# Seven-product feed-forward layers: two raw products ahead of the token sums, the sums made by halves, and the fourth layer by seven products too

## The chip, the cores and the metric

The kernel runs on one core of one Trainium2 chip. The metric is the device time of one execution in microseconds: the median of three runs of the unchanged kernel is compared with runs of the changed one. Everything is computed in fp32; a matrix product takes three matmuls, because both operands are split in a high and a low part (`hi = copy to fp32r`, `lo = x - hi`).

## The reference, cut to what matters

The network has two blocks. The change touches the second, which runs for `i = 0, 1`:

```python
def swiglu_ffn(x, w_in, w_out):
    h = x @ w_in
    g, u = jnp.split(h, 2, axis=-1)
    return (jax.nn.silu(g) * u) @ w_out

for i in range(2):
    x = layer_norm(a * x + 0.5 * swiglu_ffn(x, ffn_w_in[i, 0], ffn_w_out[i, 0]), ln_g[i, 0], ln_b[i, 0])
    h = diff_attention(x, ...) if i == 0 else pool_mixer(x, ...)
    x = layer_norm(a * x + h, ln_g[i, 1], ln_b[i, 1])
    x = layer_norm(a * x + memory_cross_attention(x, mem, ...), ln_g[i, 2], ln_b[i, 2])
    x = layer_norm(a * x + 0.5 * swiglu_ffn(x, ffn_w_in[i, 1], ffn_w_out[i, 1]), ln_g[i, 3], ln_b[i, 3])
```

There are 512 tokens, 1024 features, and 2816 hidden features, which makes 22 hidden units of 128. So there are four feed-forward layers; the text calls them F00, F01, F10 and F11, in the order in which they run. F10 stands between the two halves of the network: F01 ends just before it, and the pool mixer follows it.

## The kernel before

The engines of a core are TensorE (PE, with its weight loads PEld), VectorE (DVE), ScalarE (ACT), GpSimd (POOL) and SyncE (SP), whose queue issues nearly all loads. The kernel is written with tile pools; a planner orders each engine's instructions (by the order of the program, taking what it believes to be ready) and places the waits. Each engine then runs its list in order. Four token tiles of 128 tokens hold the activations `X`; `x_T` transposes one token tile on PE into PSUM, ACT copies the high half `xh` (L187) and DVE makes the low half `xl` (L188).

A layer is `ffn`. It works through the 22 units in chunks (6, 6, 6, 4 units, in F10 8, 7, 7). For each chunk it first makes the hidden units and then multiplies them by `w_out` into the residual, for two halves of the 1024 output columns; behind the second half of the last chunk comes the LayerNorm (`ln_tile`), one token tile after the other. Weights are made by a list of `steps`; `need(n, ahead=5)` makes all steps up to `n + ahead`: an SP load into one of three `wst` buffers (or one of four `sq`), a copy on ACT (`whi`, L168) and a subtraction on DVE (`wlo`, L169), each into one of six buffers.

Units 0 and 1 of a layer are plain: two products of 128 columns by 512 tokens each, taken in two halves of tokens, because the last token tile of `X` is still in its LayerNorm when the layer begins. `s.flush()` runs what is pending, the transpose of the last token tile, between the two halves; `finish` makes the hidden unit. In F00, F01 and F11 (`seven=True`) the other units go in pairs by a Strassen-Winograd scheme: seven products of 256 tokens with half the contraction length in place of eight. It needs sums of weights (`seven_units`: four DVE additions and seven splits a pair) and sums of tokens, made once a layer by `sums` after the flush: four additions `xh + xl` back to fp32 (L1112), four sums (L1120 to L1124), four splits (L1126, L1127). `products` issues the seven products and combines them on DVE and ACT. F10 has plain products for all units. PSUM has three banks `g`, two `a`, one `o` and two `t`.

`G` and `B`, the LayerNorm's rows, are loaded at the start of `ffn`; the constants of the pool mixer (`pool_open`: `band`, `bando`, `br`, `sr` and its own `G` and `B`) before F10 begins.

## Time and profile before

| what | us |
| --- | --- |
| median of 3 runs | 3044.82 (3042.84 to 3045.26) |
| the profiled execution, its own time | 3046.43 |
| its span, first to last instruction | 3044.6 |
| PE busy in it | 2931.4 (96%) |
| DVE busy in it | 2094.4 (69%) |
| ACT busy in it | 1262.4 (41%) |
| mean granted PE clock | 0.988 of full speed |

The span is what the trace shows; the execution's own time has a little more around it. Busy times are of instructions, and an engine that isn't on the path that sets the end may idle without cost. Matmul records overlap, since matmuls are pipelined: the distance from the start of one to the start of the next tells what one costs, not its own duration.

### The profile page before, as it was taken

What the parts mean: (1) busy time and instruction counts of PE and PEld (TensorE: products, weight loads), DVE (VectorE), ACT (ScalarE), POOL (GpSimd) and SP (SyncE); (2) the same over time, 40 slices, a digit from 0 to 9 for tenths busy, and PEclk for the clock granted to TensorE, in tenths of its full rate; (3) what the DMA queues carried; (4) which work ended last, traced back from release to release, by engine and by line L of the source; (5) the groups of instructions that cost most, each with busy time, mean ns of one, the idle gap of its engine ahead of it and who ended that gap; (6) DMA issues with size and microseconds to landing.
All of it is one profiled execution on the core that took longest, in us unless ns stands there. A gap on an engine that the chain in (4) does not pass through costs nothing.

```text
span 3044.6 us, 45001 instructions
## 1 busy us (share of the span) xinstructions
PE 2931.4 (96%) x17662; PEld 2566.0 (84%) x17662; DVE 2094.4 (69%) x3251; ACT 1262.4 (41%) x2159; POOL 434.4 (14%) x555
## 2 busy tenths in 40 slices
PE   8989999989998999999999989999999999999998
PEld 7778788878787999988888889998888888888997
DVE  6676755785766887688774687777333386687777
ACT  6435636545643344335544243333222224343332
POOL 1553510563510000011110000000000040000000
PEclk9999999999999999999999999999999999999999
DMA  5213134123132333321244233324323225223332
GB/s 187 69 57 103 39 131 164 56 61 103 46 118 82 112 117 106 96 97 57 63 147 130 79 109 91 97 91 146 103 93 95 91 77 153 70 95 100 104 97 70
DMA packets 93300, 296.99 MB, mean 98 GB/s; under 512 B 12320, under 2 KB 17952, under 8 KB 93088
## 3 DMA queue, kind: packets, MB, share of 16 engines
q1 hardware_dynamic: 92944, 293.85, 30.3%
q8 instruction: 140, 2.29, 0.3%
q14 instruction: 72, 0.59, 0.1%
q10 hardware_dynamic: 144, 0.26, 0.0%
HBM read 281.49 MB, written 12.58 MB: 97 GB/s over the span
## 4 chain that ended last, share of the span: by engine, by line
PE 74%; DVE 14%; DMA 4%; ACT 3%; issue 3%; POOL 1%; SPq 0%; DVEq 0%; ACTq 0%; POOLq 0%
PE g L176 52%; PE a L176 15%; PE o L176 5%; DVE wlo L169 3%; DVE X L283 1%; DMA wst<-in_ffn_w_in 1%; DMA wst<-in_w_in 1%; ACT whi L168 1%; PE t L246 1%; POOL rs_y L207 1%; PE t L1069 1%; DVE X L282 1%; DVE xl L188 1%; DMA sq<-in_ffn_w_in 1%; DVE nb L955 0%
## 5 line engine op out<-in xcount | busy, mean ns | idle before, releaser
L168 ACT ACTIVATE whi<-wst 128x1024 fp32r<-128x1024 f32 (+2 forms) x442 | 462.6, 1048 | 700.7 <-PE g L176 288.2
L169 DVE TENSOR_TENSOR wlo<-wst,whi 128x1024 fp32r<-128x1024 f32 (+2 forms) x435 | 535.1, 1234 | 316.2 <-ACT whi L168 301.7
L176 PE MATMUL g<-xh,whi 128*128 128x256 f32 (+1 forms) x1776 | 564.2, 318 | 2.1 <-ACT xh L187 1.5
L176 PE MATMUL g<-xl,whi 128*128 128x256 f32 (+1 forms) x1776 | 559.6, 315 | 1.3 <-DVE xl L188 1.1
L176 PE MATMUL g<-xh,wlo 128*128 128x256 f32 (+1 forms) x1776 | 559.7, 315 | 0.2 <-DVE wlo L169 0.2
L207 POOL TENSOR_TENSOR rs_y<-rs_a,mhalf 128x1 f32<-128x1 f32 (+4 forms) x90 | 99.1, 1101 | 2112.1 <-DVE rs_a L206 2110.6
L176 PE MATMUL g<-whi,xh 128*128 128x512 f32 (+2 forms) x960 | 365.5, 381 | 0.0
L176 PE MATMUL g<-wlo,xh 128*128 128x512 f32 (+2 forms) x960 | 358.7, 374 | 0.8 <-DVE wlo L169 0.8
L176 PEld LDWEIGHTS g<-xh,whi 128*128 128x128 f32 x1776 | 338.2, 190 | 23.6 <-ACT xh L187 2.9
L176 PE MATMUL g<-whi,xl 128*128 128x512 f32 (+2 forms) x960 | 358.0, 373 | 0.0
L176 PEld LDWEIGHTS g<-xh,wlo 128*128 128x128 f32 x1776 | 337.4, 190 | 21.3 <-DVE wlo L169 0.6
L176 PEld LDWEIGHTS g<-xl,whi 128*128 128x128 f32 x1776 | 337.0, 190 | 21.6 <-DVE xl L188 2.2
L176 PE MATMUL a<-xh,whi 128*128 128x256 f32 (+1 forms) x1008 | 305.1, 303 | 23.0 <-ACT xh L1126 22.6
L176 PE MATMUL a<-xl,whi 128*128 128x256 f32 (+1 forms) x1008 | 303.1, 301 | 0.0
L176 PE MATMUL a<-xh,wlo 128*128 128x256 f32 (+1 forms) x1008 | 303.0, 301 | 0.0
L168 ACT ACTIVATE whi<-sq 128x1024 fp32r<-128x1024 f32 x120 | 126.5, 1059 | 290.9 <-PE o L176 122.5
L176 PE MATMUL g<-whi,hh 128*128 128x512 f32 x547 | 217.2, 397 | 3.7 <-DVE h L1259 3.7
L176 PEld LDWEIGHTS a<-xh,whi 128*128 128x128 f32 x1008 | 194.1, 193 | 30.7 <-ACT xh L1126 23.2
L176 PE MATMUL g<-wlo,hh 128*128 128x512 f32 x547 | 216.3, 396 | 0.0
L176 PE MATMUL g<-whi,hl 128*128 128x512 f32 x547 | 216.3, 395 | 0.0
L176 PEld LDWEIGHTS g<-whi,xl 128*128 128x128 f32 x960 | 181.7, 189 | 30.4
L176 PEld LDWEIGHTS g<-wlo,xh 128*128 128x128 f32 x960 | 182.5, 190 | 29.4 <-DVE wlo L169 1.5
(389 smaller groups left out, 5602.1 us busy)
## 6 DMA issues: line engine op xcount, KB each, us to landing
wst<-in_ffn_w_in SPq DMA_DIRECT2D x146, 512.0 KB, 3.5
wst<-in_ffn_w_out SPq DMA_DIRECT2D x86, 512.0 KB, 3.6
wst<-in_w_in SPq DMA_DIRECT2D x64, 512.0 KB, 4.0
wst<-in_xa_wkv SPq DMA_DIRECT2D x32, 512.0 KB, 4.0
sq<-in_ffn_w_in SPq DMA_DIRECT2D x30, 512.0 KB, 3.5
wst<-in_da_w_qkv SPq DMA_DIRECT2D x24, 512.0 KB, 3.7
wst<-in_w_out SPq DMA_DIRECT2D x16, 512.0 KB, 3.5
wst<-in_w_pg SPq DMA_DIRECT2D x16, 512.0 KB, 4.4
```

Source lines behind the costliest of these rows:

```text
L168: s.nc.scalar.activation(hi[:, :n], st[:, :n], AF.Copy)
L169: (s.nc.gpsimd if s.lo_pool else s.nc.vector).tensor_sub(lw[:, :n], st[:, :n], hi[:, :n])
L176: s.nc.tensor.matmul(out, lhsT, rhs, start=start, stop=stop)
L188: nc.vector.tensor_sub(lo, ps, hi)
L207: nc.gpsimd.tensor_tensor(y, a, s.mhalf[:p].to_broadcast([p, n]), op=OP.pow)
L246: s.nc.tensor.transpose(ps[:, j], src[:, j * 128:(j + 1) * 128], s.ident)
L282: nc.vector.scalar_tensor_tensor(X[:, cs], X[:, cs], mv[:, 0:1], G[:, cs], op0=OP.subtract, op1=OP.mult)
L283: nc.vector.scalar_tensor_tensor(X[:, cs], X[:, cs], rs, B[:, cs], op0=OP.mult, op1=OP.add)
L1069: nc.tensor.transpose(pt[:, j], me["P"][:, j * 128:(j + 1) * 128], s.ident)
```

## The change

- `sums` gives back two functions, `fulls(z, n)` and `rest(z)`, for z = 0 and 1. Each works on half of each token half: z = 0 is token tiles 0 and 2, z = 1 is tiles 1 and 3. The intermediate sums lie in the buffers `h`, `U` and `sg` that `products` uses later, no longer in `wst` and `sq`.
- The order of the seven products becomes: both raw ones (of the two contraction halves of tokens 0 to 255) first, then four with token sums, with the raw one of tokens 256 to 511 between them. `seven_units` loads and splits the weights in that order.
- `begin` issues the two raw products of a pair. For the first pair of a layer it runs before the flush, with PSUM bank `o` for the second; after it come the sums of z = 0 and two additions of z = 1, then the flush, the rest of z = 1, the next weights, and `finish` of units 0 and 1.
- While the first units are made, weights are prepared 2 or 0 steps ahead in place of 5.
- `G`, `B` and `ST` are made at the last chunk. F10 has seven products and chunks of 6, 6, 6, 4; its work tiles lie in a pool `S` of their own on the right side of the memory, which is closed at the last chunk, and the pool mixer's constants are loaded then (`late`).

```diff
-        def full(*key):
-            f = s.stage().rearrange("p (k c) -> p k c", k=4)
-            nc.vector.tensor_add(f, *q[key])
-            return f
-
-        def summed():
-            return F.tile([128, UN], F32, name="sq", bufs=4).rearrange("p (k c) -> p k c", k=4)
-
-        st = [summed() for _ in range(4)]
-        a, b = full(0, 0), full(0, 1)
-        nc.vector.tensor_sub(st[0], a, b)
-        c = full(1, 1)
-        nc.vector.tensor_add(st[1], c, st[0])
-        nc.vector.tensor_sub(st[2], b, c)
-        nc.vector.tensor_sub(st[3], full(1, 0), st[1])
-        for n in (1, 2, 0, 3):
-            nc.scalar.activation(hi[:, n], st[n], AF.Copy)
-            nc.vector.tensor_sub(lo[:, n], st[n], hi[:, n])
+        full = [{}, {}]
+
+        def fulls(z, n):
+            zs = slice(128 * z, 128 * z + 128)
+            if n:
+                f = F.tile([128, 2, 512], F32, name="h", bufs=1).rearrange("p k (f c) -> p k f c", c=128)
+            elif z:
+                f = F.tile([128, 2, 512], F32, name="U", bufs=1).rearrange("p k (f c) -> p k f c", c=128)
+            else:
+                f = F.tile([128, 2, 2, 256], F32, name="sg", bufs=1).rearrange("p k a (b c) -> p k (a b) c", c=128)
+            for k in range(2):
+                full[z][k, n] = f[:, k]
+                nc.vector.tensor_add(f[:, k], *(y[:, :, zs] for y in q[k, n]))
+
+        def rest(z):
+            zs = slice(128 * z, 128 * z + 128)
+            f = full[z]
+            nc.vector.tensor_sub(f[0, 0], f[0, 0], f[0, 1])
+            nc.vector.tensor_sub(f[0, 1], f[0, 1], f[1, 1])
+            nc.vector.tensor_add(f[1, 1], f[1, 1], f[0, 0])
+            nc.vector.tensor_sub(f[1, 0], f[1, 0], f[1, 1])
+            for n, y in ((1, f[1, 1]), (2, f[0, 1]), (0, f[0, 0]), (3, f[1, 0])):
+                nc.scalar.activation(hi[:, n, :, zs], y, AF.Copy)
+                nc.vector.tensor_sub(lo[:, n, :, zs], y, hi[:, n, :, zs])
+
         t = [(hi[:, n], lo[:, n]) for n in range(4)]
-        return q[0, 0], t[1], t[2], t[0], q[1, 0], q[1, 1], t[3]
+        return fulls, rest, (q[0, 0], q[1, 0], t[1], t[2], t[0], q[1, 1], t[3])
...
         def u0():
             load(0, 0, s.stage())
+            return split(me[0, 0])
+
+        def u1():
+            load(0, 1, s.stage())
             load(1, 0, summed())
             load(1, 1, s.stage())
-            me["s3"] = summed()
+            return split(me[0, 1])
+
+        def u2():
+            me["s3"], me["s2"], me["s4"] = summed(), summed(), summed()
             nc.vector.tensor_add(me["s3"], me[0, 0], me[1, 0])
-            return split(me[0, 0])
-
-        def u1():
-            load(0, 1, s.stage())
-            me["s2"], me["s4"] = summed(), summed()
             nc.vector.tensor_add(me["s2"], me["s3"], me[1, 1])
             nc.vector.tensor_add(me["s4"], me["s2"], me[0, 1])
             return split(me["s2"])
 
-        def u3():
+        def u4():
             nc.vector.tensor_add(me[1, 0], me[1, 0], me[1, 1])
             return split(me[1, 0])
 
-        return [u0, u1, lambda: split(me["s3"]), u3, lambda: split(me[0, 1]), lambda: split(me["s4"]),
-                lambda: split(me[1, 1])]
-
-    def ffn(s, i, j, want_T, out=False, after=None, chunks=(6, 6, 6, 4), seven=False, room=None):
-        nc = s.nc
-        with s.scope(f"F{i}{j}") as P:
-            G, B = s.ln_rows(i, 3 * j, P)
-            ST = P.tile([128, 4, 2, 6], F32, name="ST")
+        return [u0, u1, u2, lambda: split(me["s3"]), u4, lambda: split(me["s4"]), lambda: split(me[1, 1])]
...
+    def ffn(s, i, j, want_T, out=False, late=None, chunks=(6, 6, 6, 4), room=None):
+        nc = s.nc
+        with s.scope(f"F{i}{j}") as P, ExitStack() as inside:
+            S = inside.enter_context(s.tc.tile_pool(name=f"S{i}{j}", bufs=1, side="right")) if late else P
+            hh, hl = (P.tile([128, max(chunks), 512], F32R, name=n) for n in ("hh", "hl"))
...
+            def mul(at, n, ps, ahead=5):
+
+                w = need(at + n, ahead)
+                b = ps().rearrange("p (j c) -> p j c", j=2)
+                for z in range(2):
+                    for k in range(4):
+                        s.mm3(b[:, z], tuple(x[:, k, z * 128:(z + 1) * 128] for x in w),
+                              (t7[n][0][:, k], t7[n][1][:, k]), k == 0, k == 3)
+                return b
+
+            def begin(at, ps=None, ahead=5):
+
+                p1 = S.tile([128, 2, 256], F32, name="p1", bufs=1)
+                nc.scalar.activation(p1, mul(at, 0, s.g, ahead), AF.Copy)
+                return p1, mul(at, 1, ps or s.a, ahead)
...
-                p1, U2, U3 = (P.tile([128, 2, 256], F32, name=n, bufs=1) for n in ("p1", "U2", "U3"))
-                nc.scalar.activation(p1, mul(0, s.g), AF.Copy)
-                nc.vector.tensor_sub(U2, mul(1, s.a), p1)
-                nc.vector.tensor_add(U3, mul(2, s.g), U2)
-                b = mul(3, s.a)
+                Us = S.tile([128, 2, 512], F32, name="U", bufs=1).rearrange("p n (j c) -> p n j c", j=2)
+                U2, U3 = Us[:, 0], Us[:, 1]
+                nc.vector.tensor_add(sg[:, 0], b, p1)
+                nc.scalar.activation(sg[:, 0], sg[:, 0], AF.Silu)
+                nc.vector.tensor_sub(U2, mul(at, 2, s.g), p1)
+                nc.vector.tensor_add(U3, mul(at, 3, s.a), U2)
+                b = mul(at, 4, s.g)
                 nc.vector.tensor_sub(h[:, 1], U3, b)
                 nc.vector.tensor_sub(U2, U2, b)
-                nc.vector.tensor_add(sg[:, 0], mul(4, s.g), p1)
-                nc.scalar.activation(sg[:, 0], sg[:, 0], AF.Silu)
-                nc.vector.tensor_sub(sg[:, 1], mul(5, s.a), U2)
+                nc.vector.tensor_sub(sg[:, 1], mul(at, 5, s.a), U2)
                 nc.scalar.activation(sg[:, 1], sg[:, 1], AF.Silu)
-                nc.vector.tensor_add(h[:, 0], mul(6, s.g), U3)
+                nc.vector.tensor_add(h[:, 0], mul(at, 6, s.g), U3)
...
+                if u0:
+                    hh, hl = (P.tile([128, max(chunks), 512], F32R, name=n) for n in ("hh", "hl"))
+                last = u0 + nu == FF // 128
+                begun = {}
                 if u0 == 0:
-                    for u, _, at in inner[:2]:
-                        first[u] = [part_of(at, s.g), part_of(at + 1, s.a)]
+                    first = []
+                    for u, at in inner[:2]:
+                        first.append([s.fm_part(need(at + z, 2), ps()) for z, ps in enumerate((s.g, s.a))])
                         for part in first[u]:
                             part(0, 256)
+                    fulls, rest, t7 = s.sums(room or S, S, xT)
+                    begun[2] = begin(inner[2][1], s.o, 0)
+                    fulls(0, 0)
+                    fulls(0, 1)
+                    rest(0)
+                    fulls(1, 0)
                     s.flush()
-                    if seven:
-                        t7 = s.sums(room or P, P, xT)
-                for u, by7, at in inner:
-                    if by7:
-                        products(at, hh, hl, u - u0)
-                    elif u in first:
-                        finish(hh, hl, u - u0, *(part(256, 512) for part in first[u]))
-                    else:
-                        finish(hh, hl, u - u0, *(part_of(at + z, ps)(0, 512) for z, ps in enumerate((s.g, s.a))))
-                last = u0 + nu == FF // 128
-                if last and want_T:
-                    s.new_xT()
+                    fulls(1, 1)
+                    rest(1)
+                    need(inner[2][1] + 2, 3)
+                    for u, _ in inner[:2]:
+                        finish(hh, hl, u, *(part(256, 512) for part in first[u]))
+                for u, at in inner:
+                    if u >= 2:
+                        products(at, hh, hl, u - u0, *(begun[u] if u in begun else begin(at)))
+                if last:
+                    inside.close()
+                    G, B = s.ln_rows(i, 3 * j, P)
+                    ST = P.tile([128, 4, 2, 6], F32, name="ST")
+                    if late:
+                        after = late()
+                    if want_T:
+                        s.new_xT()
...
-                with s.tc.tile_pool(name="PM", bufs=1, side="right") as P:
-                    step = s.pool_open(P)
-                    s.ffn(1, 0, False, after=step, chunks=(8, 7, 7))
+                with ExitStack() as right:
+                    step = None
+
+                    def late():
+                        nonlocal step
+                        step = s.pool_open(right.enter_context(s.tc.tile_pool(name="PM", bufs=1, side="right")))
+                        return step
+
+                    s.ffn(1, 0, False, late=late)
```

## Rows read from the trace of the kernel before

**Rows 1.** The page: the span, and its engines: busy us, share, instructions.

```profile
span 3044.6 us, 45001 instructions
...
PE 2931.4 (96%) x17662; PEld 2566.0 (84%) x17662; DVE 2094.4 (69%) x3251; ACT 1262.4 (41%) x2159; POOL 434.4 (14%) x555
```

**Rows 2.** The chain that ended last, shares of the span by engine.

```profile
PE 74%; DVE 14%; DMA 4%; ACT 3%; issue 3%; POOL 1%; SPq 0%; DVEq 0%; ACTq 0%; POOLq 0%
```

**Rows 3.** Windows: stretch, its us, then busy us of PE, PEld, DVE, ACT, POOL.

```profile
1847.43:1907.46 60.03, 60.03 (x505) 60.03 (x504) 51.10 (x54) 28.96 (x32) 0.00 (x0) 1.00 0.40 115
2357.05:2433.22 76.17, 76.17 (x337) 63.10 (x336) 26.00 (x29) 21.43 (x28) 0.00 (x0) 1.00 0.31 97
948.60:1025.14 76.54, 66.13 (x540) 65.43 (x539) 65.72 (x90) 34.18 (x43) 0.00 (x0) 0.93 0.36 110
1738.17:1812.66 74.49, 67.68 (x546) 66.75 (x544) 64.93 (x70) 32.43 (x38) 1.45 (x1) 0.95 0.38 120
2672.91:2747.94 75.03, 67.68 (x546) 66.74 (x544) 64.89 (x70) 32.43 (x38) 1.46 (x1) 0.95 0.37 119
953.94:961.55 7.61, 7.53 (x64) 7.32 (x62) 5.51 (x26) 1.80 (x3) 0.00 (x0) 1.00 0.11 16
2433.22:2462.86 29.64, 29.64 (x128) 23.80 (x127) 15.72 (x22) 5.55 (x7) 1.45 (x1) 1.00 0.28 88
```

**Rows 4.** Timeline of PE in F00, F01, F11: start, us, instruction, [idle before, releaser].

```profile
962.43 0.39 PE L176 MATMUL g<-xh,whi 128*128 128x256 f32 x1 [0.96 <-ACT xh L187]
...
986.23 1.23 PE L176 MATMUL a<-xh,whi 128*128 128x256 f32 x2 [9.38 <-ACT xh L1126]
...
1772.78 0.58 PE L176 MATMUL a<-xh,whi 128*128 128x256 f32 x1 [6.61 <-ACT xh L1126]
...
2708.07 0.58 PE L176 MATMUL a<-xh,whi 128*128 128x256 f32 x1 [6.60 <-ACT xh L1126]
...
2709.37 0.41 PE L176 MATMUL g<-xh,whi 128*128 128x256 f32 x1
2709.58 0.41 PE L176 MATMUL a<-xh,wlo 128*128 128x256 f32 x1
```

**Rows 5.** Timeline of DVE at the start of F01.

```profile
1744.72 1.28 DVE L283 SCALAR_TENSOR_TENSOR X<-X,rs_y,B 128x1024 f32<-128x1024 f32 x1 [0.44 <-POOL rs_y L207]
1751.68 0.69 DVE L188 TENSOR_TENSOR xl<-t,xh 128x512 fp32r<-128x512 f32 x1 [5.68 <-ACT xh L187]
...
1753.86 0.68 DVE L188 TENSOR_TENSOR xl<-t,xh 128x512 fp32r<-128x512 f32 x1
1754.46 1.22 DVE L1162 TENSOR_TENSOR sq<-sq,wst 128x1024 f32<-128x1024 f32 x1
1755.59 1.22 DVE L1167 TENSOR_TENSOR sq<-sq,wst 128x1024 f32<-128x1024 f32 x1
...
1778.42 1.23 DVE L1127 TENSOR_TENSOR xl<-sq,xh 128x1024 fp32r<-128x1024 f32 x1
```

**Rows 6.** Timeline of SP's queue at the start of F01.

```profile
1746.03 0.33 SPq L213 DMA_DIRECT2D G<-in_ln_g  x1
...
1746.88 0.42 SPq L1148 DMA_DIRECT2D sq<-in_ffn_w_in  x1
```

**Rows 7.** The page's costliest groups: busy us, mean ns, idle before and its releaser.

```profile
L176 PE MATMUL g<-whi,hh 128*128 128x512 f32 x547 | 217.2, 397 | 3.7 <-DVE h L1259 3.7
```

**Rows 8.** Timeline of PE, then of DVE, at the start of F10.

```profile
2101.36 1.38 PE L246 MATMUL t<-c_ident,X 128*128 128x128 f32 x8 [1.95 <-DVE xl L188]
...
2119.90 1.29 DVE L188 TENSOR_TENSOR xl<-t,xh 128x512 fp32r<-128x512 f32 x2 [6.53 <-ACT xh L187]
```

**Rows 9.** DMA issues of the whole run: times, KB each, median us to landing.

```profile
G<-in_ln_g SPq DMA_DIRECT2D x8, 512.0 KB, 4.3
...
sr<-in_pool_scale SPq DMA_DIRECT2D x1, 512.0 KB, 6.0
...
c_band<-in_band SPq DMA_DIRECT2D x1, 512.0 KB, 3.6
```

More of the change, by code (lines that the diff above doesn't have):

```diff
@@ L1141, in split, with load @@
             return tuple(x.rearrange("p (k c) -> p k c", k=4) for x in s.halves(st))
-        def part(i, k):
+        def load(i, k, st):
             f = (f0, f1)[i]
-            return s.place(key, idx, 4 * k, 4, list(range(f, f + 256)))
-        def load(i, k, st):
-            nc.sync.dma_start(st, part(i, k))
+            nc.sync.dma_start(st, s.place(key, idx, 4 * k, 4, list(range(f, f + 256))))
             me[i, k] = st
@@ L1152, in u0 @@
             load(0, 0, s.stage())
-            load(1, 0, summed())
-            load(1, 1, s.stage())
-            me["s3"] = summed()
-            nc.vector.tensor_add(me["s3"], me[0, 0], me[1, 0])
             return split(me[0, 0])
@@ L1160, in u1 @@
             load(0, 1, s.stage())
-            me["s2"], me["s4"] = summed(), summed()
+            load(1, 0, summed())
+            load(1, 1, s.stage())
+            return split(me[0, 1])
+        def u2():
+            me["s3"], me["s2"], me["s4"] = summed(), summed(), summed()
+            nc.vector.tensor_add(me["s3"], me[0, 0], me[1, 0])
             nc.vector.tensor_add(me["s2"], me["s3"], me[1, 1])
@@ L1195, in seven_in @@
                 at = len(steps)
[L1196 removed]
+                steps.extend(s.seven_units("ffn_w_in_2", (i, j), u * 128, FF + u * 128, S))
                 return at
@@ L1219, in ffn @@
                 u0 += nu
-            t7 = None
-            def part_of(at, ps):
-                return s.fm_part(need(at), ps())
             def finish(hh, hl, u, pg, pu):
-                h = P.tile([128, 2, 512], F32, name="h", bufs=1)[:, 0]
+                h = S.tile([128, 2, 512], F32, name="h", bufs=1)[:, 0]
                 nc.scalar.activation(h, pg, AF.Silu)
@@ L1780, in build @@
                     pre = s.da_open(R)
-                    s.ffn(0, 0, True, seven=True)
+                    s.ffn(0, 0, True)
                     yT = s.diff_attn(pre)
@@ L1811, in build @@
                         s.out_ln("xa_wo_2", (1,), oT, 1, 2, P, pool=R)
-                    s.ffn(1, 1, False, out=True, seven=True, room=s.xt)
+                    s.ffn(1, 1, False, out=True, room=s.xt)
                 out = True
```

28 lines of the change are left out of this document (8 added, 20 removed).

## The prediction, made before the changed kernel was run

> **What bounds the kernel now.** I read the page first. TensorE is busy for 96% of a 3044.6 us span and VectorE (DVE) for 69% [rows 1]; the chain that ended last runs through PE for 74% and DVE for 14% [rows 2]. So time is won where PE has fewer columns to stream or where it waits, and the windows say where that is. In the seven-product stage of F01, 504 matmuls of 256 columns (505 records, one over the edge) fill 60.03 us: 0.119 us each, 20.01 us a pair of units, PE never idle, DVE busy 51.10. In F10, which has plain products, seven units take 76.17 us: 10.88 a unit, 21.76 a pair, again without a gap [rows 3].
>
> The first chunks are not like that. From its first matmul to the end of chunk one, a layer with seven products has 192 half-width matmuls of the two plain units, 336 of two pairs and 16 transposes. At 0.119, and 0.10 taken for a transpose, that is 64.5 us of work. The windows are 76.54, 74.49 and 75.03 us long [rows 3]: 12.1 (F00), 10.0 (F01) and 10.6 (F11) are lost, 32.7 together. The PE timeline shows the loss: an idle of 9.38, 6.61 and 6.60 us before the first `a` product, released by ACT's `xh` at L1126, the high half of a token sum. [...] In F00 there is also 0.96 for the last token tile's transpose [rows 4].
>
> Why ACT was late is DVE's timeline in F01. It ends the LayerNorm at 1746.0, does nothing for 5.68 us, then works without a gap past 1778: weight sums, the token sums (last low half at 1778.42), splits and the two plain units' ends. In this queue 512-element operations start 0.60 apart (1753.86 to 1754.46) and 1024-element ones 1.13 (1754.46 to 1755.59) [rows 5]. The idle has two causes: all of `sums` comes after the last tile's transpose, and the first weight sum waits for `sq`, whose load SP issued at 1746.88, behind the `G` and `B` rows, which waited until 1746.03 for the old rows to be read [rows 6].
>
> **The change, part by part.** *Raw products first.* Two of the seven products need no token sum. They now come before the last tile's transpose and read only tokens 0 to 255. No matmul is added; 48 of them, 5.7 us, stand between the plain units' first halves and the transpose.
>
> *Sums by halves.* 12 wide DVE operations become 24 narrow ones: 12 x 1.13 = 13.6 us becomes 24 x 0.60 = 14.4 [rows 5], so 0.8 us of DVE more a layer. The same rows last 1.22 and 0.68 on their own, and then 14.6 becomes 16.3, 1.7 more; I take 0.8, since the queue is full there, and keep 1.7. [...]
>
> What the halving buys is that 14 of the 24 can run before the last tile. Walk F01 with the rows' distances. PE: first halves from 1738.17 to 1750.4 (96 x 0.119 + 8 x 0.10), raw products to 1756.1, transposes to 1756.9, second halves 11.4 us long. DVE from 1746.0: two low halves of raw weights 2.3, fourteen sum operations 8.4, done at 1756.7, just as the transposes end. Copy and low half of the last tile take 1.3 (DVE 0.68, ACT taken as 0.6): second halves run 1758.2 to 1769.6. DVE then needs ten more sum operations (6.0, to 1764.8) and three weight sums with one low half (4 x 1.13, to 1769.3): product three starts on time. The next weights hold DVE to 1773.8, and only then comes the multiplication that frees the PSUM bank which product four wants at 1772.5: a wait of 2.0. So 3.3 us of 10.0 remain: F01 gains 6.7. F11 is the same stage, 10.6 - 3.3 = 7.3. In F00 DVE also makes rotation tables, 5.51 us from 953.94 to 961.55 [rows 3], of which I let 1.7 delay PE: 5.0 remain, 12.1 - 5.0 = 7.1. Together **21.1 us**. Bounds: nothing but the last tile's 1.3 remains, 32.7 - 3.9 = 28.8; or the weight sums still come last, and only DVE's idle (5.7 each in F01 and F11, and I take 4 for F00) is recovered, less 1.3 and 0.8 each: 9.
>
> *`G` and `B` late.* They leave the head of the SP queue, so `sq` is no longer behind them; that is in the walk. They are now issued at the last chunk: landing takes 4.3 us [rows 9], and 48 output matmuls, 11 us at 0.233 [rows 3], run before the first row is read. Cost nothing. If that cover is gone, some 5 us a layer.
>
> *Buffers.* Sums in `h`, `U`, `sg` in place of `wst`: three load buffers are no longer held by sums. In the walk; no term of its own.
>
> *Seven products in F10.* Ten pairs x (21.76 - 20.01) = **17.5 us** gained. DVE has 13 wide and 7 narrow operations a pair, 13 x 1.13 + 7 x 0.60 = 18.9 us under 20.0, so PE still sets it, as rows 3 show it does. Three chunk ends become seven-product ends. There PE waits for DVE's `h` (L1259), 3.7 us in three layers by the page [rows 7]; 1.2 a layer; with the slower restart around each I take 2.2 for F10 (bounds 1.2 and twice that). Its own start: the first halves wait for the LayerNorm of F01 (1.95 idle at 2101.36), which stays. DVE was free for 6.53 us before the last tile's low half at 2119.90 [rows 8], room for most of the early sums, so I charge the same 3.3, less the 0.5 that the last tile cost before: 2.8 (bounds 0 and 8). F10: 17.5 - 2.2 - 2.8 = **12.5**.
>
> *The pool mixer's constants late.* `band`, `bando`, `br`, `sr` and two more rows are loaded when the right-hand pool of F10 is closed, not at its start. What is queued behind them on SP is the pool and memory weights. With 3.6 to 6 us to land [rows 9] and the first read of `G` some 14 us after the last product (60 output matmuls at 29.64/127 = 0.233 us [rows 3]), they are hidden. Two DVE operations, 1.9 us, move with them into a stretch where DVE is half free. If the memory under them is freed only by the last `hl`, 5 us later, `sr` is the last needed and still in time; else up to 4 us are lost. I take 0.
>
> Sum: 21.1 + 12.5 = 33.6. The profiled execution took 3046.43 us (span 3044.6 and 1.8 around it), the median is 3044.82, 1.6 below. 3046.4 - 33.6 = 3012.8 for a profiled run, and 1.6 less for the median: **3011 us**.
>
> **The rivals.** *DVE still sets the starts.* DVE is full from 1751.7 to 1779.6 [rows 5]; where weight sums, not token sums, end last, the starts give 9: 9 + 12.5 = 21.5, 3023 us. For it: that full queue, and 0.8 us more work in it. Against it: 5.7 us of idle DVE that the early sums fill. [...]
>
> *The starts close altogether.* If `finish` fits into gaps that DVE has while it waits for ACT's copies, 28.8 + 15 are gained: 3001 us. For it: nothing has to be faster than rows 5. Against it: PE and DVE meet within a microsecond at three points of the walk.
>
> *F10 gives nothing.* The start with its LayerNorm backlog (8), the chunk ends (2.4) and late constants (4) eat 14 of 17.5: 21 + 3, 3021 us.
>
> *Slower.* DVE becomes the bound of all 40 pairs, because the new order or the new places of the sums lengthen its operations. It has 18.9 of 20.0 us a pair; the gain of 33.6 is gone and 6 more lost once a pair takes 20.0 + 40/40 = 21.0 us. At 21.0: 3051 us. Against it: the number and size of operations in a pair stay, and rows 3 show DVE with 9 us free in three pairs.
>
> **How the numbers follow.** Within 0.2% (6.1 us) two kernels can't be told apart. Forecast as walked: 0.56, 3004 to 3018. Starts set by DVE: 0.15. Starts closed: 0.18. F10 without gain: 0.07. Slower: 0.03; no change, by other mishaps, 0.01. Range from 3000, just below the closed starts, to 3025, above the two weaker cases; it leaves out the slow case, and half of the one at 3001. Faster 0.96, same 0.01, slower 0.03.
>
> **What would show it.** The idle before the first `a` product released by a token sum's high half should be gone or under 2 us, no run of matmuls 0.21 us apart behind it; first-chunk windows of 67 to 70 us; F10's pairs 20.0 us long; DVE at work between the LayerNorm's end and the last tile's transpose; PE waits of 0.3 to 1.1 us at F10's chunk ends; no wait for `G`, `band` or `sr`. The prediction is wrong if PE waits 4 us or more at the third or fourth product, if raw products wait for their weights, or if the LayerNorm after F10 waits for a row.

## The result, and the profile after

The changed kernel takes 2999.39 us (median of 4 runs, 2995.68 to 3000.40); the kernel before, run beside it, 3045.04 (3042.84 to 3048.10). The ratio is 0.9847, 95% interval 0.9830 to 0.9864. The forecast was 3011, range 3000 to 3025: the direction and most of the size are right, the time is 0.6 us below the range, and the gain is 45.7 us where 33.6 were forecast.

The page of the changed kernel, with its chain, against [rows 1, 2, 7]:

```profile
span 2998.3 us, 46744 instructions
...
PE 2908.3 (97%) x18382; PEld 2586.4 (86%) x18382; DVE 2224.8 (74%) x3437; ACT 1305.7 (44%) x2207; POOL 431.8 (14%) x555
...
PE 14%; DVE 3%; issue 1%; DMA 0%; ACT 0%; DVEq 0%; ACTq 0%
...
L176 PE MATMUL g<-whi,hh 128*128 128x512 f32 x544 | 215.2, 396 | 0.5 <-DVE h L1266 0.5
```

PE is busy for 23 us less and idle for 23 less. The chain is no use here: its shares add up to 18%, so it was followed back through the last fifth only. The last line is the one to stop at: the wait of the output products for DVE's `h` was 3.7 us [rows 7] and is 0.5, in layers to whose chunk ends the prediction gave no term.

Windows of the changed kernel, columns as in [rows 3] (the last three are the granted clock, the DMA share and GB/s): three pairs of F01, three of F10, then the first chunks of F00, F01 and F11, and the second part (the 144 output matmuls) of F01's second chunk.

```profile
1827.65:1887.69 60.04, 60.04 (x505) 60.03 (x504) 50.89 (x54) 29.10 (x32) 0.00 (x0) 1.00 0.33 115
2183.58:2243.44 59.86, 59.86 (x506) 59.86 (x504) 50.97 (x54) 29.09 (x32) 0.00 (x0) 1.00 0.36 115
946.47:1017.38 70.91, 67.19 (x539) 66.74 (x538) 66.19 (x102) 34.50 (x47) 0.00 (x0) 0.95 0.36 118
1728.61:1793.94 65.33, 64.97 (x545) 64.48 (x544) 64.42 (x82) 32.49 (x42) 1.45 (x1) 1.00 0.38 128
2638.79:2704.15 65.36, 64.99 (x545) 64.48 (x544) 64.34 (x81) 32.30 (x41) 1.46 (x1) 1.00 0.41 128
...
1887.69:1921.15 33.46, 33.46 (x147) 27.14 (x145) 20.70 (x21) 7.42 (x7) 0.00 (x0) 1.00 0.24 79
```

Laid end to end from mark to mark of PE's timeline, the two profiled executions differ by:

| stretch | before | after | gain | forecast |
|---|---|---|---|---|
| to F00's first matmul | 948.60 | 946.47 | 2.1 | 0 |
| first chunks, F00 / F01 / F11 | 76.5 / 74.5 / 75.0 | 70.9 / 65.3 / 65.4 | 5.6 + 9.2 + 9.7 = 24.5 | 7.1 + 6.7 + 7.3 = 21.1 |
| rest of these layers, up to the next one's first part | 713.0 / 290.0 / 296.7 | 711.2 / 287.3 / 294.2 | 1.8 + 2.7 + 2.5 = 7.0 | 0 |
| F10, first part to F11's first part | 570.2 | 557.5 | 12.7 | 12.5 |

The first row is no effect: PE's instructions are the same up to there, and over the runs below that mark lies anywhere from 944.5 to 949.9 us. The third row is the term that the prediction did not have; 6.4 of its 7.0 us lie in the nine second parts of the chunks (next section).

PE and DVE at F01's start in the changed kernel, against [rows 4, 5]; the second fence is DVE:

```profile
1746.50 1.03 PE L246 MATMUL t<-c_ident,X 128*128 128x128 f32 x8
1747.79 0.39 PE L176 MATMUL g<-xh,whi 128*128 128x256 f32 x1 [0.25 <-ACT xh L187]
...
1748.64 0.38 PE L176 MATMUL g<-xl,whi 128*128 128x256 f32 x1
```

```profile
1737.07 1.29 DVE L1122 TENSOR_TENSOR sg<-xh,xl 128x512 f32<-128x512 f32 x2
...
1744.91 0.69 DVE L1133 TENSOR_TENSOR xl<-sg,xh 128x512 fp32r<-128x512 f32 x1
1745.51 1.22 DVE L1167 TENSOR_TENSOR sq<-wst,sq 128x1024 f32<-128x1024 f32 x1
...
1747.91 1.28 DVE L188 TENSOR_TENSOR xl<-t,xh 128x512 fp32r<-128x512 f32 x2
...
1757.40 1.22 DVE L169 TENSOR_TENSOR wlo<-sq,whi 128x1024 fp32r<-128x1024 f32 x1
```

The 6.61 us are gone, and with them the matmuls 0.21 us apart: from 1772.78 to 1778.12 PE's granted clock was 0.50 in the kernel before, 0.95 in the mean of F01's first chunk [rows 3], where the changed one has 1.00. DVE runs the fourteen early sums from 1737.07 to 1745.51, in 8.4 us, as walked, and two weight sums in the time that the walk left empty while ACT copies. In F00 PE still waits 2.07 and 1.66 us (966.93 and 969.33) for the last tile's halves, ACT's and DVE's. F10's start keeps its idle: 1.96 us at 2079.94, where [rows 8] have 1.95. `G`, the band and `sr` now land in 5.5, 5.1 and 6.7 us in the median [rows 9], and no matmul waits for them.

### The profile page after: what moved, and what is told of

It reads as the page before. It is cut to its first block, busy times and chain, and to the rows that moved or that the text cites. A ratio compares the mean times of both kernels' runs of the same rounds, so it can differ in the third digit from the quotient of the medians.

```text
span 2998.3 us, 46744 instructions
## 1 busy us (share of the span) xinstructions
PE 2908.3 (97%) x18382; PEld 2586.4 (86%) x18382; DVE 2224.8 (74%) x3437; ACT 1305.7 (44%) x2207; POOL 431.8 (14%) x555
## 5 line engine op out<-in xcount | busy, mean ns | idle before, releaser
L168 ACT ACTIVATE whi<-wst 128x1024 fp32r<-128x1024 f32 (+2 forms) x430 | 450.4, 1052 | 537.9 <-PE g L176 241.0
L176 PE MATMUL g<-xl,whi 128*128 128x256 f32 (+1 forms) x1936 | 588.6, 304 | 2.9 <-DVE xl L188 2.4
L176 PE MATMUL g<-xh,wlo 128*128 128x256 f32 (+1 forms) x1936 | 588.1, 304 | 0.2 <-DVE wlo L169 0.2
L176 PEld LDWEIGHTS g<-xh,whi 128*128 128x128 f32 x1936 | 369.2, 191 | 19.1 <-ACT xh L187 4.6
L176 PEld LDWEIGHTS g<-xl,whi 128*128 128x128 f32 x1936 | 368.6, 190 | 17.4 <-DVE xl L188 4.2
L176 PEld LDWEIGHTS g<-xh,wlo 128*128 128x128 f32 x1936 | 368.5, 190 | 15.0 <-DVE wlo L169 0.6
L168 ACT ACTIVATE whi<-sq 128x1024 fp32r<-128x1024 f32 x160 | 168.0, 1059 | 373.6 <-PE o L176 113.1
L176 PE MATMUL a<-xh,whi 128*128 128x256 f32 x1056 | 297.6, 282 | 0.0
L176 PE MATMUL a<-xl,whi 128*128 128x256 f32 x1056 | 297.3, 282 | 0.0
L176 PE MATMUL a<-xh,wlo 128*128 128x256 f32 x1056 | 297.3, 282 | 0.0
L169 DVE TENSOR_TENSOR wlo<-sq,whi 128x1024 fp32r<-128x1024 f32 x160 | 194.1, 1219 | 100.3 <-ACT whi L168 100.3
```

What stands on the lines that cost most here:

```text
L168: s.nc.scalar.activation(hi[:, :n], st[:, :n], AF.Copy)
L169: (s.nc.gpsimd if s.lo_pool else s.nc.vector).tensor_sub(lw[:, :n], st[:, :n], hi[:, :n])
L176: s.nc.tensor.matmul(out, lhsT, rhs, start=start, stop=stop)
```

## Experiments on the ends of the chunks

In F01 of the kernel before, the second part of a chunk begins like this (DVE, then PE):

```profile
1811.00 1.23 DVE L169 TENSOR_TENSOR wlo<-wst,whi 128x1024 fp32r<-128x1024 f32 x1 [0.33 <-ACT whi L168]
1813.71 1.23 DVE L1156 TENSOR_TENSOR sq<-wst,sq 128x1024 f32<-128x1024 f32 x1 [1.48 <-DMA wst<-in_ffn_w_in]
1814.85 0.69 DVE L1259 TENSOR_TENSOR h<-g,U 128x512 f32<-128x512 f32 x1
```

```profile
1815.59 0.50 PE L176 MATMUL g<-whi,hh 128*128 128x512 f32 x1 [0.90 <-DVE h L1259]
```

The chunk's last product ends at 1812.66. The addition L1259, which empties its bank, could start then; but DVE takes its list in order, and ahead of it stands the next chunk's first weight sum, L1156, which waits for a transfer until 1813.6. PE reaches the third `g` bank and stops. My first reading was that the change had cured this by making that sum two steps later.

**a_early** (changed kernel, from each layer's second chunk on) and **b_late** (kernel before) move the sum between steps:

```diff
 def u0():
     load(0, 0, s.stage())
+    load(1, 0, summed())
+    load(1, 1, s.stage())
+    me["s3"] = summed()
+    nc.vector.tensor_add(me["s3"], me[0, 0], me[1, 0])
     return split(me[0, 0])
```

```diff
 def u0():
...
-    me["s3"] = summed()
-    nc.vector.tensor_add(me["s3"], me[0, 0], me[1, 0])
     return split(me[0, 0])
 def u1():
     load(0, 1, s.stage())
-    me["s2"], me["s4"] = summed(), summed()
+    me["s3"], me["s2"], me["s4"] = summed(), summed(), summed()
+    nc.vector.tensor_add(me["s3"], me[0, 0], me[1, 0])
```

> The changed kernel, with the addition of the first weight sum put back into the first product's step from the second chunk of each layer on, with the two loads that it needs; the first chunks stay as changed. Theory (the chunk ends): at a chunk's end the vector engine works its queue in order, and the weight sum stands there waiting for its transfer, ahead of the addition that empties a PSUM bank; the tensor engine pays some 2.3 us at the end of the first chunk of each of F00, F01 and F11 and of F10 too: 7 to 9.5 us slower than the changed kernel, so 3006 to 3009, with waits of 0.3 to 1 us back behind the ends of the chunks. Rival (the chunk ends got shorter through the new order of the products, raw ones first): within 1 us of 2999.4.

> The kernel before, with one line moved: the first weight sum is added in the second product's step, no longer in the first's. Theory (the chunk ends): the sum no longer stands ahead of the addition that empties a bank, and 1 to 2.3 us at the end of the first chunk of each of the three seven-product layers are saved: 3038 to 3042. Rival (order of the products): no change, 3044 to 3046. A third way: all three weight sums now stand in a row, 3.4 us of the vector engine, and the wait only moves to the next addition: 3044 to 3047.

Measured: 2998.93 (changed 2999.39) and 3048.64 against 3049.09 of before in the same runs (ratio 0.9999, 0.9991 to 1.0008). In both the theory missed and the rival, no change, held: the step does not matter. On DVE's list the planner had put the sum where it stood in either kernel, ahead of the addition at eight of nine ends in b_late, at none in a_early. So the order itself was forced.

**b_behind** and **a_ahead**: `issue_after` queues an instruction behind another on its engine.

```diff
-    nc.vector.tensor_add(me["s3"], me[0, 0], me[1, 0])
+    with s.tc.issue_after(s.h_add.ins) if s.h_add else nullcontext():
+        nc.vector.tensor_add(me["s3"], me[0, 0], me[1, 0])
...
-    nc.vector.tensor_add(h[:, 0], mul(6, s.g), U3)
+    s.h_add = nc.vector.tensor_add(h[:, 0], mul(6, s.g), U3)
```

```diff
-    nc.vector.tensor_add(h[:, 0], mul(at, 6, s.g), U3)
+    b = mul(at, 6, s.g, 7 if end else 5)
+    with s.tc.issue_after(s.s3_add.ins) if end else nullcontext():
+        nc.vector.tensor_add(h[:, 0], b, U3)
```

> The kernel before, with one order forced: at a chunk's end the next chunk's first weight sum is queued right behind the addition that empties the last product's bank, where it stood ahead of it; nothing else is moved. Moving the sum to another step had left that order as it was in both kernels. Theory (the order on the vector engine is what the chunk ends cost): the second parts of the nine chunks lose what they have over 33.46 us, 7.1 us in all in the trace of before, but for the 0.1 to 0.4 that the changed kernel also shows: 5 to 7 us faster than before in the same runs. Rival (the multiplication behind the sum is late in its place, so that the wait only moves on): within 2 us of before.

> The early-sum version of the changed kernel, with the opposite order forced: at the end of each chunk but the last the addition that empties the last product's bank is queued behind the next chunk's first weight sum. Theory (the order is the cost): 0.5 to 1.3 us at each of the twelve chunk ends, 6 to 12 us slower than the changed kernel in the same runs, with the waits at the second matmuls of the chunks' second parts. Rival (the chunk ends got shorter for another reason): within 2 us.

> The changed kernel itself, unedited, as the measure for the others on the same chip: 2996 to 3001, and the difference to the early-sum kernel (2998.9) is within 2 us by both theories.

b_behind: 3040.72 against 3047.94, ratio 0.9973 (0.9962 to 0.9983): 7.2 us faster. DVE at the same place of F01 in it:

```profile
1808.50 0.69 DVE L1261 TENSOR_TENSOR h<-g,U 128x512 f32<-128x512 f32 x1 [0.63 <-PE g L176]
1809.45 1.23 DVE L1157 TENSOR_TENSOR sq<-wst,sq 128x1024 f32<-128x1024 f32 x1 [0.26 <-DMA wst<-in_ffn_w_in]
```

All nine second parts now take 33.60 to 33.61 us, where those of before have 33.60 to 34.77: 5.8 us less together. The rest isn't placed with certainty; in the trace of b_behind F10's start, whose instructions the edit leaves alone, also ran 2.1 us faster (92.02 for 94.16), at a granted clock of 1.00 for 0.97 (last section). a_ahead: 3001.48 against 2999.50 of the changed kernel, which ran unedited beside it as **a_again**: 2.0 us, a miss for 6 to 12. There the addition came late at all twelve ends, yet PE mostly did not stop. Its list in a_ahead, at the second chunk of F00, from the second part's start at 1111.22 (6 `g`, then all three `o`, then twelve `g`), beside DVE:

```profile
1111.22 0.39 PE L176 MATMUL g<-whi,hh 128*128 128x512 f32 x1
...
1113.08 0.39 PE L176 MATMUL o<-whi,hl 128*128 128x512 f32 x1
1113.32 0.39 PE L176 MATMUL g<-whi,hh 128*128 128x512 f32 x1
```

```profile
1111.52 1.23 DVE L1161 TENSOR_TENSOR sq<-wst,sq 128x1024 f32<-128x1024 f32 x1 [0.71 <-DMA wst<-in_ffn_w_in]
1112.67 1.22 DVE L169 TENSOR_TENSOR wlo<-wst,whi 128x1024 fp32r<-128x1024 f32 x1
1113.80 0.68 DVE L1276 TENSOR_TENSOR h<-g,U 128x512 f32<-128x512 f32 x1
```

With the addition planned late, the planner also gave PE other work to reach first; `h` starts 2.6 us after the chunk's last product, and nothing waits there; PE stopped at three of the twelve ends, for 0.68 to 0.84 us. The order cost time where PE's list counted on the addition and a transfer delayed it, as in F01 above: 0.90 us of idle behind 1.48 that DVE waited for the load.

What in the change removed it? **a_order** takes a version with the starts undone (a_all_undone, below) and puts back one thing more, the order of the seven products with the weight steps that go with it:

```diff
-return [u0, u1, u2, lambda: split(me["s3"]), u4, lambda: split(me["s4"]), lambda: split(me[1, 1])]
+return [u0, u2, lambda: split(me["s3"]), u4, lambda: split(me[0, 1]), lambda: split(me["s4"]), lambda: split(me[1, 1])]
...
-return fulls, rest, (q[0, 0], q[1, 0], t[1], t[2], t[0], q[1, 1], t[3])
+return fulls, rest, (q[0, 0], t[1], t[2], t[0], q[1, 0], q[1, 1], t[3])
```

> The version with all three undone at the starts, and the order of the seven products put back as before too (the first weight sum's product second, the raw product of the third and fourth token sets fifth). Theory A (what that version still kept of the starts' gain, 12.3 us of 24.5, is the order: the first product that needs a token sum is the third and no longer the second, one product of 2.9 us more of cover at each start): 3019 to 3023. Theory B (it is the buffers of the token sums): 3008 to 3013.

3017.89 against 3010.78: 7.1 us slower, between its two theories, and not at the starts (next section). DVE in it, where F00's second chunk passes from its products to its second part, at 1117.39:

```profile
1117.60 1.23 DVE L1157 TENSOR_TENSOR sq<-wst,sq 128x1024 f32<-128x1024 f32 x1 [0.62 <-DMA wst<-in_ffn_w_in]
1118.74 0.68 DVE L1264 TENSOR_TENSOR h<-g,U 128x512 f32<-128x512 f32 x1
```

The sum is ahead again, at nine of twelve ends. Sums over 33.46 us (the shortest there is) of the nine second parts in F00, F01 and F11: before 7.1, b_behind 1.3, changed 0.7, a_all_undone 0.1, a_order 5.5. So the rival of the first run was right about the origin: the order of the products decides where the planner puts the sum. Why its plan turns on that is not shown.

## Experiments on the starts

Each undoes parts of what the change does at a layer's start, or adds them to the kernel before.

**a_full** (the first edit; `fulls` and `rest` are then the same operations at full width), **a_raw_late** (the second), **a_full_raw_late** (both):

```diff
-fulls(0, 0)
-fulls(0, 1)
-rest(0)
-fulls(1, 0)
 s.flush()
-fulls(1, 1)
-rest(1)
+fulls()
+rest()
```

```diff
-begun[2] = begin(inner[2][1], s.o, 0)
 fulls(0, 0)
...
 rest(1)
+begun[2] = begin(inner[2][1], s.o, 0)
```

> The changed kernel, with the token sums at full width, all after the last token tile, and no longer by halves; the raw products stay first and the weight sums stay late. Theory (the halves carry the larger part of what the starts gained): twelve operations of some 1.13 us follow the last tile's normalization where ten of 0.60 did, 7.5 us, of which the high halves and the finish cover some: 2 to 5 us at each of the four starts, 3007 to 3019. Rival (the raw products alone cover the sums): 2999 to 3002.

> The changed kernel, with the two raw products of each start behind the token sums and no longer ahead of the last token tile; sums by halves as changed. Theory (the raw products carry a part of the starts): the tensor engine has 5.7 us less to do while the last tile is normalized, so 3 to 5 us of each of the starts of F01, F10 and F11 come back, and 0 to 5 of F00: 9 to 20 us slower than the changed kernel. Rival (the sums are what counts, and the raw products cover as much behind them as ahead of the tile): within 3 us.

> The changed kernel with two things undone together at the starts: token sums at full width behind the last token tile, and the raw products behind the sums; the weight sums and the weights' loads stay late. Theory A (the parts add up): 6.4 for the width and -4.7 for the order of the raw products, as each measured alone: 3000 to 3003. Theory B (each covers for the other, and with neither the tensor engine waits for the whole row of sums): 3010 to 3022.

**a_w_early** (weights ahead, with the first weight sum back in a pair's first step; rest as changed), **a_all_undone** (all three), **b_tiles** (the sums of before made in place in `sg`, `h`, `U` and one `wst`), **b_tiles_late** (and the weights late, with the first weight sum in a pair's second step):

```diff
-first.append([s.fm_part(need(at + z, 2), ps()) for z, ps in enumerate((s.g, s.a))])
+first.append([s.fm_part(need(at + z), ps()) for z, ps in enumerate((s.g, s.a))])
...
-begun[2] = begin(inner[2][1], s.o, 0)
+begun[2] = begin(inner[2][1], s.o)
```

```diff
-first[u] = [part_of(at, s.g), part_of(at + 1, s.a)]
+first[u] = [part_of(at, s.g, 1), part_of(at + 1, s.a, 1)] if seven else [part_of(at, s.g), part_of(at + 1, s.a)]
...
 t7 = s.sums(room or P, P, xT)
+need(inner[2][2] + 1, 0)
```

> The changed kernel with the weights put back ahead at the starts: up to five steps ahead as in the kernel before, where the changed kernel takes two and none, and the first pair's weight sums in its first two steps; sums by halves and raw products first stay. Theory A (what the starts gained over the halves is the late weights: in the kernel before the weight sums and halvings stand among the token sums on the vector engine): 10 to 18 us slower than the changed kernel, 3009 to 3018. Theory B (the order of the weights is free at the starts): within 3 us of 2999.5.

> All three undone at the starts together (weights ahead, sums at full width behind the last tile, raw products behind them); what stays of the change there is that the token sums are made in place in tiles of their own, where those of before took the staging and sum buffers that the weights need. Theory A (order and width are the starts): the 24 us come back, 3019 to 3025. Theory B (the buffers carry a part: weights could not be loaded while the token sums held them): 3005 to 3015.

> The kernel before, with its token sums made in place in tiles of their own and one staging buffer, where they took four sum buffers and four turns of the three staging buffers; order, width and weights as before. Theory A (order of the products): within 3 us of before. Theory B (buffers: the token sums had to wait until the weight sums that held the same buffers were split): 8 to 12 us faster than before.

> The kernel before with the token sums in tiles of their own and, at the starts, weights no more than one step ahead, the weight sums traced behind the token sums; order of the products and width of the sums as before. Theory (late weights alone are the largest part of what the starts gained): 15 to 20 us faster than the version with own tiles alone in the same runs, most of it in the first chunks of F00, F01 and F11. Rival (they pay only together with the new order of the products): within 3 us of it.

**a_late_order**: a_full_raw_late with the products in the order of before.

> The changed kernel with sums at full width behind the last tile and raw products behind them (2993.8), and now the order of the seven products as before, the first weight sum's product second; the weights stay late. Theory A (with late weights the order decides some 5 us at the starts of F01, F10 and F11, since the second product already waits for a weight sum and a token sum; the chunk ends cost 4 to 7 more, as they did with weights ahead): 3010 to 3016. Theory B (the order is only worth the chunk ends): 2998 to 3002.

| kernel | median | ratio to before, 95% | first chunks F00 / F01 / F11 | sum |
|---|---|---|---|---|
| before, beside the changed kernel | 3045.04 | | 76.5 / 74.5 / 75.0 | 226.0 |
| b_tiles | 3045.28 | 0.9988 (0.9979 to 0.9996) | 74.6 / 74.5 / 75.1 | 224.2 |
| b_tiles_late | 3026.81 | 0.9927 (0.9914 to 0.9941) | 70.9 / 69.9 / 70.8 | 211.6 |
| a_w_early | 3023.43 | 0.9919 (0.9905 to 0.9932) | 75.2 / 72.3 / 72.0 | 219.4 |
| a_order | 3017.89 | 0.9899 (0.9886 to 0.9913) | 74.5 / 68.7 / 68.3 | 211.5 |
| a_all_undone | 3010.78 | 0.9879 (0.9866 to 0.9893) | 73.3 / 69.6 / 70.9 | 213.8 |
| a_late_order | 3006.34 | 0.9858 (0.9841 to 0.9874) | 70.8 / 64.9 / 65.2 | 200.8 |
| a_full | 3005.85 | 0.9861 (0.9846 to 0.9876) | 71.6 / 67.5 / 67.4 | 206.5 |
| a_again | 2999.50 | 0.9841 (0.9828 to 0.9854) | 69.3 / 65.4 / 65.0 | 199.6 |
| a_raw_late | 2994.79 | 0.9826 (0.9813 to 0.9840) | 66.7 / 64.9 / 64.9 | 196.5 |
| a_full_raw_late | 2993.76 | 0.9826 (0.9813 to 0.9839) | 69.8 / 64.8 / 64.8 | 199.4 |

The kernel before ran beside each group, with medians from 3047.66 to 3049.09, and each ratio is to its own. Both measures at the starts that the title names can be taken out, and the kernel is 5.7 us faster than a_again. Alone, full width costs 6.4, between theory and rival, and late raw products gain 4.7, which neither side of a_raw_late expected; for both together theory A's sum, 3001, was a miss of 7 on the good side, since the parts do not add up. Late weights are the large term: put back ahead they cost 24 us with halves (a_w_early, more than its theory A allowed) and 17.0 without (a_all_undone against a_full_raw_late), and in the kernel before they gain 18.5 as medians (b_tiles to b_tiles_late, as expected); the two profiled executions differ by 12.0, with 12.6 at the three starts. The buffers alone give 2.7, so a_all_undone fell into its theory B's range, but not for theory B's reason.

DVE and PE at F01's start in a_w_early show why:

```profile
1747.96 1.22 DVE L1176 TENSOR_TENSOR sq<-sq,wst 128x1024 f32<-128x1024 f32 x1
1749.10 1.22 DVE L1181 TENSOR_TENSOR sq<-sq,wst 128x1024 f32<-128x1024 f32 x1
1750.23 1.22 DVE L1177 TENSOR_TENSOR sq<-sq,wst 128x1024 f32<-128x1024 f32 x1
1751.37 1.22 DVE L169 TENSOR_TENSOR wlo<-sq,whi 128x1024 fp32r<-128x1024 f32 x1
...
1757.85 1.28 DVE L188 TENSOR_TENSOR xl<-t,xh 128x512 fp32r<-128x512 f32 x2
```

```profile
1754.22 0.28 PE L176 MATMUL a<-xh,whi 128*128 128x256 f32 x1
1758.59 0.58 PE L176 MATMUL g<-xl,whi 128*128 128x256 f32 x1 [4.08 <-DVE xl L188]
1758.97 0.42 PE L176 MATMUL g<-xh,wlo 128*128 128x256 f32 x1
```

The last tile's low half is ready to be made when ACT has copied it at 1753.7, and is made at 1757.85, behind weight sums and token sums that no matmul needs yet. PE loses 4.08 us and goes on with matmuls 0.21 us apart in place of 0.12. In the kernel before, the same work stands one place later, behind the tile's low half [rows 5] and ahead of the first token sum, L1112:

```profile
1756.72 1.22 DVE L1163 TENSOR_TENSOR sq<-sq,wst 128x1024 f32<-128x1024 f32 x1
1757.86 2.35 DVE L169 TENSOR_TENSOR wlo<-sq,whi 128x1024 fp32r<-128x1024 f32 x2
1760.13 1.22 DVE L1112 TENSOR_TENSOR wst<-xh,xl 128x1024 f32<-128x1024 f32 x1
```

From 1754.46 to 1760.13 three weight sums and two low halves of weights take 5.7 us, and three more low halves follow before the token sum whose high half ends PE's idle of 6.61. In a_full_raw_late the tile's low half comes at once; two of the twelve full-width operations run ahead of it, the other ten behind:

```profile
1734.22 1.22 DVE L1119 TENSOR_TENSOR sg<-xh,xl 128x1024 f32<-128x1024 f32 x1
...
1738.87 1.23 DVE L1119 TENSOR_TENSOR wst<-xh,xl 128x1024 f32<-128x1024 f32 x1
1740.02 1.28 DVE L188 TENSOR_TENSOR xl<-t,xh 128x512 fp32r<-128x512 f32 x2
1741.22 1.22 DVE L1119 TENSOR_TENSOR h<-xh,xl 128x1024 f32<-128x1024 f32 x1
...
1753.70 1.22 DVE L1129 TENSOR_TENSOR xl<-wst,xh 128x1024 fp32r<-128x1024 f32 x1
```

From 1740.0 to 1754.9 is 14.9 us; the second halves (11.4) and the two raw products (5.7) are 17.1 us of PE, all now behind the tile. Raw products ahead of it cover a wait that hardly exists.

The order of the products is worth little at the starts: with weights ahead the old one is 2.3 us shorter (a_order against a_all_undone), with late weights 1.4 longer (a_late_order against a_full_raw_late). (a_late_order as a whole, 3006.34, lies between its two theories.) That leaves the step from b_tiles_late (211.6) to a_late_order (200.8), and the like one from b_tiles to a_order (12.7), nearly all of both in F01 and F11: in the `a_` kernels the pair's first two products, and the call for the weights behind them, are traced ahead of the plain units' ends, in the `b_` ones behind them, and the second product has bank `o`. At F01's start in b_tiles_late PE waits 1.68 us for the high half of a weight (ACT, L168) and 1.46 us for the addition of a plain unit (DVE, L1224) before the first product in bank `a`; a_late_order has neither wait. That fits, but no run moved these things alone, so these 11 us are argued, not shown.

## Experiments on F10, the rows and F00's tables

**a_f10_plain** gives F10 plain products in chunks of 8, 7, 7; **a_rows_early** puts `G`, `B` and `ST` back at the head of `ffn`:

```diff
-s.ffn(1, 0, False, late=late)
+s.ffn(1, 0, False, late=late, chunks=(8, 7, 7), seven=False)
```

```diff
+            G, B = s.ln_rows(i, 3 * j, P)
+            ST = P.tile([128, 4, 2, 6], F32, name="ST")
             xT = s.xT
...
                     inside.close()
-                    G, B = s.ln_rows(i, 3 * j, P)
-                    ST = P.tile([128, 4, 2, 6], F32, name="ST")
```

> The changed kernel, with F10 alone computed by plain products in chunks of 8, 7 and 7 as before; its gains, its pool constants and its buffers stay late. Theory (the seven products pay in F10 what the prediction's term says, 12.5, and what was moved to the layer's end is free): 3011 to 3013. Rival (part of F10's 12.7 comes from the loads and constants that are now made at its end): 3004 to 3009. Other rival (they cost something at the end, which the products had to earn first): 3014 or more.

> The changed kernel, with the gains, the biases and the statistics tile of each layer allocated and loaded at the layer's start again. Theory (the loads' place is free, as the prediction has it): within 2 us of 2999.5. Rival (at the start they stand in the queue of loads ahead of weights that the first products need): 2 to 6 us slower.

a_f10_plain: 3015.19 (0.9889, 0.9875 to 0.9902), 16.3 above a_early of the same runs; the two profiled executions differ by 14.3. From the transposes ahead of F01's last two output matmuls to F11's first part the traces have 573.1 us for it, 561.5 for a_early and 562.3 for the changed kernel: the products are worth 10.8 to 11.6, the rest lies where both run the same instructions. By its time this is the case of the other rival, that what moved to F10's end costs something there; but from F10's first part to F11's the plain F10 takes 568.3 us here, with late constants, and 568.3 in b_behind and b_tiles, with early ones. The late constants are free.

F10's end costs something all the same. PE behind the last output matmul of F10 in the changed kernel:

```profile
2434.52 2.05 PE L176 MATMUL t<-c_band,X 128*128 128x128 f32 x16 [1.55 <-DVE X L283]
```

The pool mixer's transposes wait for the LayerNorm's `X`, 1.55 us here, then 2.83 and 2.77, and the mean granted clock from 2432.8 to 2490.0 is 0.88. From the start of F10's last second part to F11's first part the changed kernel takes 228.4 us and a_f10_plain 240.1, of which 16.8 are 72 more output matmuls at 0.233: the changed kernel loses 5.1 us there. In a_f10_plain the first of these transposes run among the last output matmuls. That the shorter last chunk, four units in place of seven, covers less of the LayerNorm is argued; no run changed the chunks alone.

a_rows_early: 2999.65, no cost and no gain, as its theory had it.

**best1** and **best2** add to a_raw_late and a_full_raw_late that F00 makes the rotation tables at its end, as F10 does with its constants:

```diff
-with s.tc.tile_pool(name="DP", bufs=1, side="right") as R:
-    pre = s.da_open(R)
-    s.ffn(0, 0, True)
+with ExitStack() as right:
...
+    s.ffn(0, 0, True, late=late)
     yT = s.diff_attn(pre)
```

> The changed kernel with the raw products behind the sums, and in F00 the rotation tables and the constants of the attention that follows made at the layer's end, as F10 does with its pool constants. Theory (the tables and their waits for transfers, some 8 us of the vector engine ahead of F00's token sums, are the 2.2 us that F00's first chunk still loses there): 2992 to 2994. Rival (at the layer's end they cost as much): 2995 to 2999.

> The changed kernel with token sums at full width behind the last tile, raw products behind them, and F00's tables made at the layer's end. Theory (the tables were what F00's first chunk still waited for, here 5 us of it): 2988 to 2991. Rival (they cost at the layer's end what they save at its start): 2992 to 2995.

2992.87 (0.9819, 0.9805 to 0.9832) and **2989.53** (0.9806, 0.9793 to 0.9820), both as their theories expected. F00's first chunk in best2 has no idle left, and best2 is the fastest version here, 10 us below the change:

```profile
949.74:1013.63 63.89, 63.89 (x539) 63.89 (x538) 60.21 (x64) 32.01 (x39) 0.00 (x0) 1.00 0.40 131
```

## Why the prediction was right and where it failed

**The chunk ends of F00, F01 and F11 failed.** The prediction read the wait for L1259 in [rows 7], charged it to F10 as a new cost of 2.2 (measured: F10's second parts are 34.21, 33.60 and 33.60 us, so about 0.6; the 1.0 in it for a slower restart was an estimate; in the kernel before the second part of F01's first chunk, with 0.90 of idle, takes 34.77, 1.3 over the shortest), and gave the layers that already paid it no term. There the change gained 7.0, 6.4 of it at the nine second parts, through the new order of the products; b_behind gets 5.8 at the same places out of the kernel before by forcing that order on DVE alone. Counting only first chunks as changed was the error: the order of seven products is new in every pair.

**The starts were under-sized, and their cause was wrong.** 24.5 for 21.1. In F01 the walk's times for early sums and transposes hold, but its 2.0 at product four did not come, nor most of the 1.3 for the last tile: 0.8 of 3.3 remains, 0.9 in F11; F00 keeps 6.4 where 5.0 were allowed. "What the halving buys" was the wrong step: a kernel without it, and without raw products first, has starts as short. What the runs show in its place, for about half of the gain, is that weight sums and low halves of weights left DVE's list ahead of the last tile's low half and of the token sums: 12.6 us at the three starts in the kernel before (b_tiles to b_tiles_late), 14.4 in the changed one (a_all_undone to a_full_raw_late). The other 11 stay open, as said above. The prediction listed this work in [rows 5] and feared it, in the rival with 3023; it never priced its move as the gain. Its sign, first chunks of 67 to 70 us, was missed on both sides: 65.3, 65.4 and 70.9.

**F10** came out at 12.7 for 12.5 by luck, with its parts wrong in pairs. The pairs take 19.95 us, as forecast, and the chunk ends cost 0.6 for 2.2, but the LayerNorm behind its last product, which the prediction had at nothing, costs 5.1: the products give 10.8 to 11.6, not 12.5. Another 2.0 come from its start, where the kernel before ran at a granted clock of 0.97 (94.16 us for the first chunk) and others with the same plain F10 at 1.00 (92.02 in b_behind). **Rows, constants and buffers at nothing** hold: a_rows_early 0.2 us, no wait for the pool's constants; of the buffers, own tiles alone gave 2.7, 1.9 of it in F00's first chunk. The rival at 3001, starts closed altogether, was nearest in time, by luck: two of its three starts closed, and the chunk ends, which it did not have, made up for the third. What would make the prediction wrong, waits of 4 us at products or rows, did not occur.

**The halving itself** cost what the prediction took for it: the fourteen early halves start 0.60 us apart, 8.4 us in all, and the full-width operations of a_full_raw_late 1.13 to 1.14 apart, which makes the 0.8 a layer. DVE's busy time agrees in kind but can't tell 0.8 from the 1.7 that the single durations give: 2221.0 us at full width, 2224.8 and 2227.7 (a_again) in two executions of the changed kernel, which is 0.95 or 1.7 a layer.

## What to carry to other kernels

At the start of a stage, look at what stands in an in-order engine's list ahead of the one operation that the bound engine needs, and first move what nobody needs yet; splitting needed work into pieces comes after that (here late weights gave the kernel before 12.6 us at three starts). Where a bank is emptied by an engine that also prepares the next stage, check that no operation waiting for a transfer is queued ahead of the one that empties it, and force the order (b_behind: 5.8 us at nine ends), since the place in the program may not decide it (b_late: no change). When a change alters the order of a repeated unit, price every end and seam of it, not only the place that the change is about.

## What the runs showed that I had not expected

The same matmuls ran at different granted clocks. After F01, PE idles 1.95 us in the kernel before and 1.96 in the changed one; F10's plain first chunk then ran at a mean granted clock of 0.97 in before and b_late (94.16 and 94.06 us), 0.96 in b_tiles_late (94.38), and at 1.00 in b_behind, b_tiles and a_f10_plain (92.02, 92.02, 92.01). No run tells what decides it. And up to F00's first matmul PE's instructions are the same in the two kernels, while that mark moved by 5.4 us over the runs: a span differs by that much without a cause in the change, so a few us are to be read from the stage concerned.
